# A two-layer backbone on one core: centred values, guards in place of four waits for transfers, and other prices for transfers in the kernel's planner

## The chip, the cores and the metric

The kernel runs on one core of a Trainium2 chip. A core has TensorE (PE in the profile; its weight loads are the row PEld), VectorE (DVE), ScalarE (ACT), GpSimd (POOL) and SyncE (SP), each with a queue of its own that is worked off in order, and 16 DMA engines. DMAs of this kernel are issued by SP and POOL. The metric is device time in microseconds (us), the median of several runs.

## The reference

The model has two layers over 512 tokens (x) and a context of 256 tokens, of width 1024. Layer 0 is an RWKV-7 mixer with a scan forwards and backwards over 32 heads of 64, layer 1 a Hyena mixer with long convolutions. What matters here, cut down:

```python
def adaln(cond, w, b):
    return jnp.split(jax.nn.silu(cond) @ w + b, 3, axis=-1)

def rwkv7_scan(...):            # per head, S is 64 x 64
    s = s * w_t + (s @ a_t) b_t + v_t k_t ;  y_t = s @ r_t

def rwkv7_readout(y, bonus, gate, p, dtype):
    mean = jnp.mean(y, axis=-1, keepdims=True)
    var = jnp.mean(jnp.square(y - mean), axis=-1, keepdims=True)
    yn = merge_heads((y - mean) * lax.rsqrt(var + RWKV_GN_EPS))
    yn = yn * p['ln_w'] + p['ln_b']
    return ((yn + merge_heads(bonus)) * jax.nn.silu(gate)).astype(dtype)

def hyena_filters(length, p):   # three sine layers of width 64, then f_w4 and a window
    hdn = sin(...) ; filt = hdn @ p['f_w4'] ; return filt * window
```

The output y of the scan is linear in the values v, along the 64 channels over which the readout takes its mean: the mean of y is what the same scan would give for the mean of v.

## The kernel before, in words

The order of the instructions is worked out while the kernel is built. Generators (each a piece of the work: a product, a readout, a chain) sit in lanes; `run` (L255) asks each live generator for its next instruction, and emits the one that a model of the chip (class Model, L72) lets start first. A lane's `bias` is added to that time, so that a negative one brings its work forward. `Model.note` (L142) keeps a clock for each engine and one clock `mem` for all transfers: a transfer of `size` elements takes size / 62e3 us on it and lands 0.6 us later. The chip does not know these clocks: each engine runs its instructions in the order of emission, and waits where one is not ready. A generator that yields nothing waits in the plan without an instruction being emitted.

The stages in the profile: up to 240 us the norm, adaln's first parts and the products for the values; from 240 to 740 us the products for keys, r and gates, decays, the key side and a part of the triangular inverses; then the scan, and beside it the readouts and the output product; from 1606 us the last readouts, the filters of layer 1 and the residual; then layer 1.

- `adaln` (L478) computes silu(c) times the weights, in blocks of columns. In the lane `mods1` it takes 128 columns at a time, in two loads of four row blocks each into one buffer `aw`: load, four matmuls into a PSUM bank of kind `ad`, load, four more, one more with the bias, a copy, and a second use of the bank. From the scan on, kind `ad` is the same single bank as kind `pm` (L1283), which the merges, the readouts and filter_base use as well. The bank is held from the first matmul to the copy, across the second load.
- `inverse` (L1229) loads blocks of the triangular systems by six transposing DMAs (lt<-ld, pieces of 32 elements) and works on them on DVE.
- `merge` (L1325) puts the inverses of one pair of heads together; the chain of a round (two pairs) needs its two merges.
- `chain` (L1483) is the scan: 8 rounds of 12 steps, each four groups of small matmuls with copies between them. `fetch` and `prep` (L1372, L1410) bring its operands (ar, bk) and, for the first group of a pair, transpose the values by matmuls with `ident` (L1425).
- `gemms` with `g_out` (L943) makes the gates; each product is emptied by the lane `evac` (L881). From the scan on one PSUM bank serves them.
- `readout` (L1568) takes y of one pair: product with `mean64` for the mean, subtraction, square, product with `mean64` for the variance, Ln, Exp, multiplications, then the bonus and the gate. `operand` and `out_part` make the output product of it.
- `filter_base` (L580) computes the three sine layers during the scan and stores them to DRAM (`hkd`). After the scan `filter_loads` (L560) loads f_w4 and the windows, `filter_parts` (L612) loads hkd twice into one tile, rounds it (ACT), takes the remainder (DVE) and multiplies, and `filter_transforms` makes the filter's transform.

Of the kernel before, what the change touches and what calls it, by code (L numbers as in the profile page):

```python
# [17 lines left out]
P = 128  # L18
# [20 lines left out]
for _n, _w in [("sel", 2), ("one32", 32), ("ones", 128), ("selg", 128), ("ident", 128), ("mean64", 128), ("ones64", 128), ("mask", 256),  # L39
               ("scanm", 12 * 65)]:  # L40
    CST[_n] = (_o, _w)
    _o += _w
# [29 lines left out]
class Model:  # L72
# [41 lines left out]

    def free(self, eng, ap, write):
# [26 lines left out]
    def note(self, op):  # L142
# [3 lines left out]
        if fn == "dma_start":  # L146
# [6 lines left out]
            self.mem = max(self.mem, go + 0.9) + size / 62e3  # L153
            end, e = self.mem + 0.6, "D"
# [85 lines left out]
def net_kernel(ctx: ExitStack, tc: tile.TileContext, I, out, dbg=None):  # L240
# [188 lines left out]
    ident, ones, mean64, ones64 = K("ident"), K("ones"), K("mean64"), K("ones64")  # L429
# [47 lines left out]

    def adaln(lps, ap, width, nk, bufs, row, aw=None):  # L478

        todo = [(l, part, cb, k) for l, part in lps for cb in range(D // width) for k in range(0, KT, nk)]  # L480
        w = []

        def load(l, part, cb, k):
            t = aw(len(w)) if aw else tl(ap, "aw", [P, nk, width], bufs)
            w.append(t)
            src = I["ada_w"][l, k * P:(k + nk) * P, part * D + width * cb:part * D + width * (cb + 1)]
# [3 lines left out]
        for n, (l, part, cb, k0) in enumerate(todo):  # L490
# [4 lines left out]
            if n + bufs - 1 < len(todo):  # L495
                yield load(*todo[n + bufs - 1])
            if k0 == 0:
                b, t = yield from get("ad")
                b = b[:, 0:width]
            for k in range(k0, k0 + nk):  # L500
# [44 lines left out]
    hkd = tl(dr, "hkd", [64, TX])  # L545
# [14 lines left out]
    def filter_loads():  # L560

        w4 = I["l1_f_w4"].rearrange("k (b c) -> k b c", b=2)
        for i, cb in funits:
# [8 lines left out]
            floads.append((wf, wft, win))  # L572
# [7 lines left out]
    def filter_base():  # L580
# [27 lines left out]
        yield dma(out=hkd, in_=hd)  # L608
# [3 lines left out]
    def filter_parts():  # L612
# [3 lines left out]
        hk, hd = filter_tile("hk", [P, TX], dt=F32R), filter_tile("hd", [P, TX], tag="ev")  # L616
        for hf in range(2):
            yield dma(out=hd[64 * hf:64 * hf + 64], in_=hkd)
        yield S.activation(out=hk, in_=hd, func=AF.Copy)
        yield V.tensor_tensor(out=hk[64:128], in0=hd[64:128], in1=fr(hk[64:128]), op=SUB)  # L620
        for n, (i, cb) in enumerate(funits):
            while len(floads) <= n:
                yield
            wf, wft, win = floads[n]
# [785 lines left out]
    def prep(p, g):  # L1410
# [6 lines left out]
        if g == 0:  # L1417
            vw, VT, vtok = vals[p]
            for c0 in range(0, NC, 8):
                n = min(8, NC - c0)  # L1420
                b, t = yield from get("pb")
                for i in range(n):
                    for h in range(2):
                        yield T.matmul(b[HR[1 - h], i * C:(i + 1) * C], lhsT=vw[:, (c0 + i) * C:(c0 + i + 1) * C], rhs=ident[:, HR[h]], start=True, stop=True)
# [143 lines left out]
    def readout(p, yb):  # L1568
# [10 lines left out]
        b, t = yield from get("pm")  # L1579
        yield T.matmul(b, lhsT=mean64, rhs=y, start=True, stop=True)  # L1580
        yield V.tensor_tensor(out=y, in0=y, in1=b, op=SUB)
        t[0] = True
# [502 lines left out]
```

## Time and profile before

| what | us |
|---|---|
| median of 3 runs | 2297.0 (2293.72 to 2299.8) |
| the profiled execution | 2309.6 |
| its span | 2307.7 |
| PE busy | 2032.2 (88%) |
| DVE busy | 1650.6 (72%) |
| ACT busy | 1058.7 (46%) |
| mean granted clock of PE | 0.941 of full speed |

The profile shows one execution. The span is the time from its first to its last instruction. A busy time is the time in which an engine executes; what an engine waited for is inferred from its semaphores. An fp32 matmul of 128 columns by 512 appears as two records. A wait for a transfer (DMA) is named by the tile that is loaded and the tensor that it comes from, as aw<-ada_w. PE and its weight loads are listed apart, and a stall often shows in both.

### The profile page before, as it was taken

Reading aid. Unit: us, or ns where it says so; the run is one execution under the profiler, and the core shown is the slowest. Engines: PE = TensorE matmul, PEld = TensorE weight load, DVE = VectorE, ACT = ScalarE, POOL = GpSimd, SP = SyncE. Lnnn points to the kernel's source line nnn. Section 1 sums busy time; section 2 is a strip of 40 time slices with the busy share of each in tenths; the row PEclk is TensorE's granted clock in tenths of the full one; section 3 lists DMA queues with packets and bytes.
Section 4 is the critical chain, followed back from the end, with each engine's and each line's share of the span. In section 5 each row is a group of like instructions: output and inputs, shape, how many; then the busy total and the mean of one; then the engine's idle time right before and its main releaser. Section 6 shows DMA issues by size and latency. Waiting matters only on the chain.

```text
span 2307.7 us, 53374 instructions
## 1 busy us (share of the span) xinstructions
PE 2032.2 (88%) x21710; PEld 1606.1 (70%) x21710; DVE 1650.6 (72%) x2646; ACT 1058.7 (46%) x1881; POOL 375.8 (16%) x583
## 2 busy tenths in 40 slices
PE   6699899999877688788988988888779999999997
PEld 2488777777655466666777767776457788878786
DVE  1956379989789678856676766776677676758676
ACT  2534578879663233334444443533563333333333
POOL 0400100000000432323334242211232000000000
PEclk8699999999989897989999999999889999999999
DMA  7145757795777975668655556453575323233232
GB/s 244 43 174 187 235 177 244 249 261 182 227 218 267 181 201 131 151 159 174 147 151 145 139 147 154 133 149 92 181 214 178 131 70 110 78 96 96 85 123 76
DMA packets 317564, 369.26 MB, mean 160 GB/s; under 512 B 132387, under 2 KB 203630, under 8 KB 317320
## 3 DMA queue, kind: packets, MB, share of 16 engines
q1 hardware_dynamic: 303832, 330.34, 49.6%
q0 software_dynamic: 13488, 35.52, 5.3%
q8 instruction: 171, 2.80, 0.5%
q14 instruction: 73, 0.60, 0.1%
HBM read 262.79 MB, written 102.17 MB: 158 GB/s over the span
## 4 chain that ended last, share of the span: by engine, by line
PE 52%; DVE 19%; DMA 12%; issue 5%; ACT 3%; SPq 2%; POOL 1%; DVEq 0%; ACTq 0%; POOLq 0%
PE ps L58 52%; SPq L58 2%; DVE wlo L58 2%; DVE bk L58 2%; DVE ar L58 2%; DMA aw<-ada_w 2%; DMA ar<-zd 2%; DMA wraw<-wg 2%; DVE ltm L58 1%; DVE ta L58 1%; DVE sv L58 1%; DVE lt L58 1%; DMA ar<-ard 1%; DVE cvv L58 1%; DMA tt<-td 1%
## 5 line engine op out<-in xcount | busy, mean ns | idle before, releaser
L58 PE MATMUL ps<-m,whi 128*128 128x512 f32 (+1 forms) x1536 | 423.3, 377 | 35.1 <-DVE ro L58 11.2
L58 ACT ACTIVATE whi<-wraw 128x512 fp32r<-128x512 f32 x320 | 200.8, 628 | 388.6 <-PE ps L58 274.8
L58 DVE TENSOR_TENSOR wlo<-wraw,whi 128x512 fp32r<-128x512 f32 x320 | 225.8, 707 | 200.8 <-ACT whi L58 198.6
L58 PEld LDWEIGHTS ps<-m,whi 128*128 128x128 f32 x1536 | 264.7, 197 | 92.1 <-ACT m L58 13.5
L58 PE MATMUL ps<-m,wlo 128*128 128x512 f32 (+1 forms) x768 | 247.7, 373 | 4.9 <-DVE wlo L58 4.8
L58 PE MATMUL ps<-ar,bk 128*64 128x64 f32 (+2 forms) x4096 | 220.2, 243 | 31.6 <-DVE ar L58 11.9
L58 PEld LDWEIGHTS ps<-ar,bk 128*64 128x64 f32 (+1 forms) x4096 | 186.7, 141 | 54.4 <-issue 22.0
L58 PE MATMUL ps<-h1h,whi 128*128 128x512 f32 x512 | 201.4, 393 | 2.6 <-ACT whi L58 1.9
L58 PE MATMUL ps<-h1l,whi 128*128 128x512 f32 x512 | 200.2, 391 | 0.7 <-DVE h1l L58 0.7
L58 PE MATMUL ps<-h1h,wlo 128*128 128x512 f32 x512 | 200.6, 392 | 0.0
L58 PEld LDWEIGHTS ps<-m,wlo 128*128 128x128 f32 x768 | 134.1, 197 | 31.5 <-DVE wlo L58 6.7
L58 DVE TENSOR_TENSOR ar<-ps,cst 64x512 f32<-64x512 f32 (+1 forms) x192 | 115.1, 600 | 28.3 <-PE ps L58 22.3
L58 POOL TENSOR_TENSOR sc<-sc,gam 128x256 f32<-128x256 f32 x80 | 55.5, 694 | 421.6 <-DVE sv L58 413.5
L58 PEld LDWEIGHTS ps<-h1h,whi 128*128 128x128 f32 x512 | 96.3, 188 | 22.5 <-ACT whi L58 2.3
L58 PEld LDWEIGHTS ps<-h1h,wlo 128*128 128x128 f32 x512 | 96.4, 188 | 20.3 <-DVE wlo L58 0.7
L58 PEld LDWEIGHTS ps<-h1l,whi 128*128 128x128 f32 x512 | 96.3, 188 | 20.3 <-DVE h1l L58 1.2
L58 PE MATMUL ps<-sv,bt 128*64 128x64 f32 x1408 | 90.7, 238 | 12.1 <-DVE sv L58 6.4
L58 ACT ACT_TABLE_LOAD x75 | 96.2, 1283 | 5.2 <-PE ps L58 3.1
L58 DVE TENSOR_TENSOR ltm<-lt 128x90 f32<-128x90 f32 (+14 forms) x120 | 81.1, 676 | 20.8 <-DMA lt<-ld 17.5
L58 PEld LDWEIGHTS ps<-sv,bt 128*64 128x64 f32 x1408 | 68.6, 143 | 38.6 <-ACT sv L58 14.1
L58 PE MATMUL ps<-xs,tt 128*64 128x64 f32 x1536 | 68.5, 233 | 28.6 <-DVE xs L58 26.7
L58 POOL DMA_DIRECT2D tt<-td x144 | 87.1, 609 | 9.9 <-DMA zd<-tt 4.9
(292 smaller groups left out, 4382.6 us busy)
## 6 DMA issues: line engine op xcount, KB each, us to landing
wraw<-wg SPq DMA_DIRECT2D x128, 256.0 KB
wraw<-w SPq DMA_DIRECT2D x128, 256.0 KB
aw<-ada_w SPq DMA_DIRECT2D x96, 256.0 KB
bkd<-bk SPq DMA_DIRECT2D x32, 768.0 KB
ard<-ar SPq DMA_DIRECT2D x32, 640.0 KB
ar<-ard SPq DMA_DIRECT2D x128, 128.0 KB
ar<-zd SPq DMA_DIRECT2D x128, 128.0 KB
wraw<-w_out SPq DMA_DIRECT2D x64, 256.0 KB
```

What stands on the lines that cost most here:

```text
L58: return getattr(self.eng.eng, self.fn)(*self.a, **self.k)
```

## The change

- The transposition of the values multiplies by `cent` = I - mean over each head's 64 channels, in place of I. Values and y are then centred; the readout's product for the mean and its subtraction are left out, and the variance's product takes `ones64` with a scale of 1/64 in the Ln.
- `adaln` remembers for each load the PE clock of the plan plus 8.0 us, and (but in its early use) yields nothing until that clock is reached: before it takes the bank, and before each group of matmuls.
- `filter_base` makes the rounded half and the remainder of the sine layers itself and stores both; `filter_parts` has one load, on POOL's queue, and neither ACT's nor DVE's instruction. Its first unit also yields nothing until 9.0 us of the plan's PE clock after the first weights' load.
- Transfers are priced by the length of their contiguous pieces (the shorter of the two sides): 27e3 elements per us up to 32 elements, 50e3 up to 64, 66e3 beyond, and each lands 1.2 us later.
- The lane `evac` has the bias -0.5 from the scan on.

```diff
@@ -36,7 +36,7 @@
 
 CST = {}
 _o = 0
-for _n, _w in [("sel", 2), ("one32", 32), ("ones", 128), ("selg", 128), ("ident", 128), ("mean64", 128), ("ones64", 128), ("mask", 256),
+for _n, _w in [("sel", 2), ("one32", 32), ("ones", 128), ("selg", 128), ("ident", 128), ("cent", 128), ("ones64", 128), ("mask", 256),
                ("scanm", 12 * 65)]:
     CST[_n] = (_o, _w)
     _o += _w
@@ -112,6 +112,16 @@
                 hi += s * (n - 1)
         return p0, p0 + pn, lo, hi
 
+    @staticmethod
+    def run(ap):
+
+        n = 1
+        for s, m in reversed(ap.ap if ap.space == DRAM else ap.ap[1:]):
+            if s != n and m > 1:
+                break
+            n *= m
+        return n
+
     def free(self, eng, ap, write):
         tr = self.tracks.get(self.key(ap))
         if not tr:
@@ -150,8 +160,9 @@
                 self.hw = max(self.hw, start) + 0.53
                 self.clock[e], go = start + 0.06, self.hw
             size = min(math.prod(outs[0].shape), math.prod(ins[0].shape)) if ins else 0
-            self.mem = max(self.mem, go + 0.9) + size / 62e3
-            end, e = self.mem + 0.6, "D"
+            run = min(self.run(v) for v in (*outs, *ins))
+            self.mem = max(self.mem, go + 0.9) + size / (27e3 if run <= 32 else 50e3 if run <= 64 else 66e3)
+            end, e = self.mem + 1.2, "D"
         else:
             end = self.clock[e] = start + self.price(e, op, outs[0], start)
             if outs[0].shape[0] < P:
@@ -426,7 +437,7 @@
         o, w = CST[name]
         return cst[:, o:o + w]
 
-    ident, ones, mean64, ones64 = K("ident"), K("ones"), K("mean64"), K("ones64")
+    ident, ones, cent, ones64 = K("ident"), K("ones"), K("cent"), K("ones64")
     mask = K("mask").rearrange("p (z a t) -> p z a t", z=2, a=2)
     par = tl(con, "par", [P, len(PAR), NP])
     do(dma(out=par, in_=I["par"]))
@@ -475,14 +486,17 @@
     do(V.tensor_scalar(out=cth, in0=cth, scalar1=0.5, scalar2=0.5, op0=MUL, op1=ADD))
     do(V.tensor_tensor(out=cpad[:, :, 0:2], in0=c2, in1=cth, op=MUL))
 
+    AWL = 8.0
+
     def adaln(lps, ap, width, nk, bufs, row, aw=None):
 
         todo = [(l, part, cb, k) for l, part in lps for cb in range(D // width) for k in range(0, KT, nk)]
-        w = []
+        w, at = [], []
 
         def load(l, part, cb, k):
             t = aw(len(w)) if aw else tl(ap, "aw", [P, nk, width], bufs)
             w.append(t)
+            at.append(model.clock["T"] + AWL)
             src = I["ada_w"][l, k * P:(k + nk) * P, part * D + width * cb:part * D + width * (cb + 1)]
             return dma(out=t, in_=src.rearrange("(k p) c -> p k c", p=P))
         for t in todo[:bufs - 1]:
@@ -494,9 +508,13 @@
                 yield dma(out=adab, in_=I["ada_b"][l:l + 1, part * D + width * cb:part * D + width * (cb + 1)])
             if n + bufs - 1 < len(todo):
                 yield load(*todo[n + bufs - 1])
+            while not aw and k0 == 0 and model.clock["T"] < at[n]:
+                yield
             if k0 == 0:
                 b, t = yield from get("ad")
                 b = b[:, 0:width]
+            while not aw and model.clock["T"] < at[n]:
+                yield
             for k in range(k0, k0 + nk):
                 yield T.matmul(b[32 * (k % 4):32 * (k % 4) + 32, :], lhsT=cpad[:, k, :], rhs=w[n][:, k - k0], start=k < 4, stop=k > 4)
             if k < KT - 1:
@@ -542,7 +560,7 @@
     td = [[tl(dr, f"td{z}_{b}", [2, UB, 32, 32]) for b in range(NB)] for z in range(2)]
 
 
-    hkd = tl(dr, "hkd", [64, TX])
+    hkd = tl(dr, "hkd", [P, TX])
     kfd = [tl(dr, f"kfd{b}", [P, 2, 4, 512]) for b in range(4)]
 
     def filter_tile(name, shape, bufs=1, dt=F32, tag=None):
@@ -569,7 +587,7 @@
             for hf in range(2):
                 yield FQ.dma_start(out=wf[64 * hf:64 * hf + 64], in_=w4[:, :, cs])
             win = []
-            floads.append((wf, wft, win))
+            floads.append((wf, wft, win, model.clock["T"] + 9.0))
             for a in range(4):
                 while winring.full():
                     yield
@@ -605,7 +623,11 @@
             yield V.scalar_tensor_tensor(out=hd, in0=nn, scalar=-6.28125, in1=hd, op0=MUL, op1=ADD)
             yield V.scalar_tensor_tensor(out=hd, in0=nn, scalar=-(2 * math.pi - 6.28125), in1=hd, op0=MUL, op1=ADD)
             yield S.activation(out=hd, in_=hd, func=AF.Sin)
-        yield dma(out=hkd, in_=hd)
+        hh = tl(rv, "hh", [64, TX], dt=F32R, tag="vx")
+        yield S.activation(out=hh, in_=hd, func=AF.Copy)
+        yield dma(out=hkd[0:64], in_=fr(hh))
+        yield V.tensor_tensor(out=hd, in0=hd, in1=fr(hh), op=SUB)
+        yield dma(out=hkd[64:128], in_=hd)
         toks[0][0] = toks[1][0] = True
         fbase.append(1)
 
@@ -613,15 +635,12 @@
 
         while not fbase:
             yield
-        hk, hd = filter_tile("hk", [P, TX], dt=F32R), filter_tile("hd", [P, TX], tag="ev")
-        for hf in range(2):
-            yield dma(out=hd[64 * hf:64 * hf + 64], in_=hkd)
-        yield S.activation(out=hk, in_=hd, func=AF.Copy)
-        yield V.tensor_tensor(out=hk[64:128], in0=hd[64:128], in1=fr(hk[64:128]), op=SUB)
+        hk = filter_tile("hk", [P, TX], dt=F32R)
+        yield G.dma_start(out=hk, in_=hkd.bitcast(F32R))
         for n, (i, cb) in enumerate(funits):
-            while len(floads) <= n:
+            while len(floads) <= n or (n == 0 and model.clock["T"] < floads[0][3]):
                 yield
-            wf, wft, win = floads[n]
+            wf, wft, win, _ = floads[n]
             sw = wf[:, 0, :]
             yield V.tensor_tensor(out=sw, in0=wf[:, 0, :], in1=wf[:, 1, :], op=SUB if i else ADD)
             swh, swl = filter_tile("swh", [P, 512], dt=F32R), filter_tile("swl", [P, 512], dt=F32R)
@@ -1415,13 +1434,14 @@
             yield
         AR, BK, ARB, BT, tok, btok = got_[p, g]
         if g == 0:
+
             vw, VT, vtok = vals[p]
             for c0 in range(0, NC, 8):
                 n = min(8, NC - c0)
                 b, t = yield from get("pb")
                 for i in range(n):
                     for h in range(2):
-                        yield T.matmul(b[HR[1 - h], i * C:(i + 1) * C], lhsT=vw[:, (c0 + i) * C:(c0 + i + 1) * C], rhs=ident[:, HR[h]], start=True, stop=True)
+                        yield T.matmul(b[HR[1 - h], i * C:(i + 1) * C], lhsT=vw[:, (c0 + i) * C:(c0 + i + 1) * C], rhs=cent[:, HR[h]], start=True, stop=True)
                 yield copy((V, S), VT[:, c0:c0 + n], b[:, 0:n * C].rearrange("p (c d) -> p c d", d=C))
                 t[0] = True
             vtok[0] = True
@@ -1576,15 +1596,11 @@
         yield dma(out=vx, in_=vd[p][:, SX])
         yield G.tensor_tensor(out=bo, in0=bo, in1=vx, op=MUL)
         y = yb[:, p % 2].rearrange("p c t -> p (c t)")
-        b, t = yield from get("pm")
-        yield T.matmul(b, lhsT=mean64, rhs=y, start=True, stop=True)
-        yield V.tensor_tensor(out=y, in0=y, in1=b, op=SUB)
-        t[0] = True
         s2 = tl(rv, "s2", [P, TX])
         yield S.activation(out=s2, in_=y, func=AF.Square)
         b, t = yield from get("pm")
-        yield T.matmul(b, lhsT=mean64, rhs=s2, start=True, stop=True)
-        yield S.activation(out=s2, in_=b, func=AF.Ln, bias=gneps)
+        yield T.matmul(b, lhsT=ones64, rhs=s2, start=True, stop=True)
+        yield S.activation(out=s2, in_=b, func=AF.Ln, scale=1.0 / 64, bias=gneps)
         t[0] = True
         yield S.activation(out=s2, in_=s2, func=AF.Exp, scale=-0.5)
         yield V.tensor_tensor(out=y, in0=y, in1=s2, op=MUL)
@@ -1680,6 +1696,7 @@
     G2BIAS = 0
     EPW = 0
     glane.bias = G2BIAS
+    evac.bias = -0.5
     pick["eps"] = EPW
     run([Lane([(passed, bring.out[:], rings["pb"].toks[2])]), Lane([(zeros,)]), *scans, *ends], lambda: over(glane, evac))
     gpc.close()
@@ -1995,7 +2012,7 @@
     put("ident", np.eye(P))
     put("ones", 1.0)
     same = (i[:, None] // 64 == i[None, :] // 64)
-    put("mean64", same / 64.0)
+    put("cent", np.eye(P) - same / 64.0)
     put("ones64", same)
     s, t = i[:, None] % 64, np.arange(64)[None, :]
     put("mask", np.concatenate([s < t, s <= t, s > t, s >= t], 1))
```

## Rows read from the trace of the kernel before

**Rows 1.** The page: the span, and busy time and share of each engine.

```profile
span 2307.7 us, 53374 instructions
...
PE 2032.2 (88%) x21710; PEld 1606.1 (70%) x21710; DVE 1650.6 (72%) x2646; ACT 1058.7 (46%) x1881; POOL 375.8 (16%) x583
```

**Rows 2.** Busy time by stage: stretch, length, engines (instructions), PE clock, DMA share, GB/s.

```profile
240.00:740.00 500.00, 449.81 (x3554) 343.80 (x3552) 425.54 (x568) 358.88 (x612) 15.78 (x51) 0.95 0.73 230
...
740.00:852.00 112.00, 83.67 (x941) 64.17 (x943) 78.41 (x125) 33.66 (x57) 46.24 (x60) 0.87 0.82 196
...
852.00:1606.00 754.00, 657.29 (x13318) 527.98 (x13315) 537.53 (x1016) 309.40 (x624) 227.84 (x381) 0.95 0.59 143
...
1606.00:1720.00 114.00, 75.65 (x296) 52.96 (x290) 76.21 (x114) 58.74 (x98) 32.66 (x28) 0.82 0.65 196
...
1850.00:2308.00 458.00, 439.65 (x2123) 366.53 (x2121) 314.79 (x517) 151.85 (x257) 5.39 (x4) 0.99 0.29 92
```

**Rows 3.** Waits of PE, whole run: total us, times, longest us.

```profile
PE ps L58 <- DMA aw<-ada_w: 31.3, 13, 12.8
```

**Rows 4.** Waits of PE for transfers from 240 to 740 us.

```profile
PE ps L58 <- DMA aw<-ada_w: 9.1, 7, 3.8
```

**Rows 5.** Waits of PE, then of DVE, from 740 to 852 us.

```profile
PE ps L58 <- DMA aw<-ada_w: 12.8, 1, 12.8
...
PE ps L58 <- DVE ro L58: 11.2, 4, 5.5
...
DVE ltm L58 <- DMA lt<-ld: 14.8, 1, 14.8
```

**Rows 6.** Waits of PE for transfers from 852 to 1606 us.

```profile
PE ps L58 <- DMA aw<-ada_w: 9.4, 5, 3.9
...
PE ps L58 <- DMA ar<-zd: 7.8, 8, 1.5
...
PE ps L58 <- DMA ar<-ard: 4.5, 3, 1.8
...
PE ps L58 <- DMA bk<-bkd: 3.5, 1, 3.5
```

**Rows 7.** Timeline after the scan: start, us, engine, instruction [idle before, releaser].

```profile
1609.85 1.11 SPq L58 DMA_DIRECT2D hd<-hkd  x2
...
1619.60 0.63 ACT L58 ACTIVATE hk<-hd 128x512 fp32r<-128x512 f32 x1 [14.54 <-DMA hd<-hkd]
...
1622.98 1.22 PE L58 MATMUL ps<-s,cst 128*128 128x512 f32 x1 [14.16 <-ACT s L58]
```

**Rows 8.** DMA issues: queue, count, KB each, median us to landing.

```profile
tfl<-fcl POOLq DMA_DIRECT2D x1, 512.0 KB, 8.8
```

**Rows 9.** Groups of instructions by shape: count, busy us, mean ns, idle before.

```profile
L58 PE MATMUL ps<-yb,cst 128*128 128x512 f32 x32 | 17.9, 642 | 2.0 <-ACT tt L58 1.8 <-DVE npo L58 0.2
...
L58 DVE TENSOR_TENSOR yb<-yb,ps 128x512 f32<-128x512 f32 x16 | 10.9, 680 | 0.6 <-PE ps L58 0.4
```

**Rows 10.** Timeline of the last readout.

```profile
1634.53 1.84 PE L58 MATMUL ps<-yb,cst 128*128 128x512 f32 x2
...
1638.36 0.63 ACT L58 ACTIVATE s<-yb 128x512 f32<-128x512 f32 x1 [1.95 <-DVE yb L58]
```

**Rows 11.** Timeline of SP's queue at the change of stage.

```profile
750.96 9.61 SPq L58 DMA_DIRECT2D lt<-ld  x6
...
762.81 0.39 SPq L58 DMA_DIRECT2D aw<-ada_w  x1
```

**Rows 12.** Timeline before the first step of the chain.

```profile
806.68 0.43 PE L58 MATMUL ps<-aw,cpad 128*32 128x128 f32 x8
...
823.75 0.15 DVE L58 SCALAR_TENSOR_TENSOR sc<-ps,npre 128x2 f32<-128x2 f32 x1
...
837.91 1.19 PE L58 MATMUL ps<-t,l 32*32 32x32 f32 x96
...
852.38 0.34 PE L58 MATMUL ps<-xs,tt 128*64 128x64 f32 x4
```

## The prediction

> **What bounds the kernel now.** I read the page first, then the busy times by stage, then the waits of TensorE (PE) stage by stage, then the timelines of the two places where PE stands longest. The page says that PE is busy for 88% of the span and VectorE (DVE) for 72% [rows 1]: no engine is full, so the stage decides. The table by stage [rows 2] shows four regimes. From 240 to 740 us (keys and decays) PE is busy for 449.8 of 500 us and DVE for 425.5: two engines share the bound, and a stall of one can hide behind the other. From 740 to 852 us (change to the scan) PE is busy for 83.7 of 112 us and its granted clock is 0.87. From 852 to 1606 us (the scan's chain, 96 steps) PE is busy for 657.3 of 754 us: 96.7 us of gaps, in a stage in which each step waits for the one before it. From 1606 to 1720 us (last readouts, filters, residual) PE is busy for 75.7 of 114 us, at a granted clock of 0.82. From 1850 us on PE is busy for 439.7 of 458 us at 0.99; the change leaves no operation out there, and I count nothing for it.
>
> Since every engine takes its instructions in the planner's order, an instruction that the planner believes ready and that is not stops all that is queued behind it. The waits for adaln's weight tile are of that kind: PE stands 31.3 us in 13 waits [rows 3].
>
> **The change part by part.** The sum is made in the profiled execution, 2309.6 us with what lies around its span of 2307.7 us [rows 1]; the median of the runs shown is 2297.0, so 12.6 us are taken off at the end.
>
> *Guards in adaln.* No instruction is added; the planner only withholds the matmuls until its PE clock is 8 us past the load's issue, so other PE work is put ahead. Of the 31.3 us, 9.1 lie between 240 and 740 us [rows 4], 12.8 in one wait between 740 and 852 us [rows 5], 9.4 in the scan [rows 6]. In the first stage DVE is 85% busy [rows 2], so a PE that runs earlier often finds DVE late next: I take 4 us (0 to 9.1). In the scan the chain's own small matmuls sit behind the stalled one, and little covers it: I take 7 (0 to 9.4). The 12.8 us wait is partly SP's doing: SP issues lt<-ld for 9.61 us from 750.96, and the load of aw goes out only at 762.81 [rows 11]. The planner counts its 8 us from where it thinks the load was issued, so the guard can miss some of it.
>
> *Prices.* Transfers in pieces of at most 32 elements go from 62 to 27 thousand elements per us, of at most 64 to 50, longer ones to 66, and each lands 0.6 us later. The six lt<-ld loads (65,536 elements each) were priced at 6 x 1.06 = 6.3 us and are now 6 x 2.43 = 14.6; on the chip DVE stood 14.8 us for them [rows 5]. So the planner will put other work ahead of that inverse. In the scan PE stands 7.8 + 4.5 + 3.5 = 15.8 us for ar and bk [rows 6]; those of ar are long pieces, whose price moves by 0.6 us only. I take 5 of the 15.8. A new order can also lose; no row prices that, and I bound it at 10 us in the scan, about a tenth of its 96.7 us of gaps.
>
> *evac.bias = -0.5 from the scan's start.* The evacuation of a gate tile is picked sooner on ScalarE (ACT) and DVE. PE stood 11.2 us in four waits for DVE's ro [rows 5], since one PSUM bank serves these products. With the 12.8 us this makes 24.0 us between 740 and 852 us. But this stage ends at the chain's first step, and what sets that is not PE: the second merge needs the one PSUM bank of kind pm, which adaln held from 806.68 to 823.75 us; the merge's first matmul came at 837.91, the chain's at 852.38 [rows 12]. I take 6 us, from 24.0 down to a loss of 17.1, one more such hold (806.68 to 823.75) ahead of the merge.
>
> *Centred values.* The values' transposing matmuls take another constant of the same shape: no cost. Each of 16 readouts loses one fp32 product (two records in the trace) and one DVE subtraction: 17.9/16 = 1.12 us of PE and 10.9/16 = 0.68 us of DVE [rows 9]. ACT's Ln takes a scale in place of the scaled constant: nothing. 14 readouts lie in the scan: 15.7 us of PE, off the chain itself but between its steps on the same queue. With PE 87% busy there I take half, 8 us (0 to 15.7). In the last readout they lie on the path: from the product at 1634.53 to the square at 1638.36 are 3.8 us [rows 10]; I take 3.
>
> *The filter's basis.* After the scan ACT waits 14.54 us for hd<-hkd, which SP issues behind the filter's own loads, and the readout's square stands behind it in ACT's queue: PE's next matmul comes after 14.16 us of nothing [rows 7]. Now the split is made long before, in filter_base (one ACT copy and one DVE subtraction of half a tile, at most 0.63 + 0.68 us by like rows [rows 7, 9], taken as nothing, in the chain's gaps; 1.3 if not), two stores go out where one did, and one load on POOL's queue brings hk. ACT and DVE no longer wait for it; PE does, and behind that the filter. A load that POOL issued there landed in 8.8 us [rows 8], so hk is there at about 1606 + 1 + 9 = 1616 us in place of 1619.60 + 0.63 = 1620.2: the filter gains 4 us, the readouts up to 14.2. The readouts lead to the output product and the residual, the filter has work to spare: nearer the 14.2, I take 10 (4 to 14.2). The guard on the first filter weights (9 us) ends at about the same time as the load and costs nothing more.
>
> A page speaks against part of this. The Trainium skill, "DMA: Bandwidth & Descriptors", section "Issuing engines are not separate DMA queues", says that transfers issued by SP, ACT or POOL run on the same 16 DMA engines and interleave. By that rule hk, with the filter's other loads in flight, would land no sooner than hd did; no row of before has this load on POOL. The sum would lose most of the 10 us (third rival).
>
> **The sum.** 4 (240 to 740) + 6 (740 to 852) + 7 + 5 + 8 = 20 (scan) + 10 + 3 = 13 (after it) = 43 us. 2309.6 - 43 = 2266.6, less 12.6: **2254 us**. All bounds at their best: 9.1 + 24.0 + 40.9 + 18.0 = 92 us, 2205; all at their worst: 0 - 17.1 - 10 + 4 - 1.3 = a loss of 24, 2321.
>
> **The rivals.**
> First, *other waits take over*: PE's stalls were cover for DVE, which is then late itself. For it: DVE is busy for 425.5 of 500 us and 78.4 of 112 us [rows 2]. Against it: the 14 us after the scan are idle on every engine. Gain 2 + 0 + 10 + 10 = 22 us: 2275.
> Second, *the prices do more*: most transfer waits of the scan go (9.4 + 15.8 us) with all of the readout's share (15.7), and the change of stage gives 12: 4 + 12 + 36 + 13 = 65 us, 2232.
> Third, *hk lands as late as hd did* and the filter binds after the scan: 1 + 3 = 4 us in place of 13, 34 in all: 2263.
> Fourth, *nothing much*: two stages give a little, a later start of the chain takes it back: 2297.
> Fifth, on the other side, *adaln keeps the bank*. A guarded second half holds pm for at least 8 us after its load is issued. The hold in the trace is 17.1 us [rows 12]; filter_base, the first two merges and the readouts want the same bank. If more holds fall ahead of the second merge, the chain starts later by 17.1 us each. The other gains are 4 + 20 + 13 = 37 us: from three holds on (51 us) it is slower. Four: 68 - 37 = 31 us lost, 2328; three: 2311. I price it at 2315. For it: two loads lie in each hold. Against it: this hold already had a load in it, and planned holds grow by a few us only.
>
> **How the numbers follow.** Forecast 2254 (2240 to 2268): 0.45. First rival 0.22, second 0.12, third 0.08, fourth 0.05, fifth 0.08. Runs of this kernel differ by about 0.3%, 7 us. Faster by more than that: 0.45 + 0.22 + 0.12 + 0.08 = 0.87; within: 0.05; slower: 0.08. The range takes in the first three rivals and stops below the fourth: 2224 to 2294.
>
> **What would show it.** PE's waits for aw after 240 us under 10 us; no wait of ACT for hd<-hkd and less than 9 us of PE idle after the scan; 32 records fewer of ps<-yb,cst; the chain's first step by 848 us and its 96 steps in under 740 us; ps<-m matmuls no longer waiting for ro. The prediction is wrong if the chain starts after 870 us, if adaln ends so late that the residual waits for it, or if the gaps of PE in the scan stay near 97 us.

## The result and the profile after

The changed kernel takes 2330.8 us (median; 2324.9 to 2335.0) where the kernel before takes 2298.4 beside it: 1.0122 times as long, 95% interval 1.0099 to 1.0145. It is slower, and the forecast of 2254 us and the range of 2224 to 2294 both miss. The profiled execution has a span of 2331.8 us, 24.1 more than before [rows 1]; the medians differ by 32.4 us, since the profiled execution of before, 2309.6 us, lies 11.2 above its median.

The page of the kernel after: the span, and busy time and share of each engine.

```profile
span 2331.8 us, 53247 instructions
...
PE 2028.5 (87%) x21678; PEld 1610.2 (69%) x21678; DVE 1650.6 (71%) x2633; ACT 1067.9 (46%) x1908; POOL 356.7 (15%) x555
```

PE has 32 records fewer than before and is busy 3.7 us less, so its idle time grew by 27.8 us. But the 32 records took 17.9 us [rows 9]: the records that stay took 14.2 us longer, at a mean granted clock of 0.934 in place of 0.941. The run a65 below makes the same 21,678 records in another order:

```profile
PE 2016.7 (88%) x21678; PEld 1602.1 (70%) x21678; DVE 1646.3 (72%) x2626; ACT 1070.0 (47%) x1906; POOL 367.6 (16%) x564
```

So a part of after's loss is PE busy for longer with the same work; the rest is waiting. How much of that part belongs to the order is open: f_cent and f_both below, of nearly one order, are busy for 2026.4 and 2017.5 us.

The stages of the kernel after, cut at the same events as in [rows 2] (columns as there).

```profile
240.00:750.00 510.00, 445.88 (x3503) 344.28 (x3502) 428.14 (x563) 357.15 (x613) 16.66 (x49) 0.94 0.70 220
750.00:868.00 118.00, 92.20 (x1017) 70.21 (x1015) 86.52 (x142) 38.24 (x64) 42.37 (x56) 0.87 0.86 209
868.00:1641.00 773.00, 653.81 (x13232) 526.90 (x13232) 520.07 (x990) 314.44 (x644) 215.95 (x361) 0.92 0.56 140
1641.00:1755.00 114.00, 76.54 (x313) 54.97 (x312) 82.13 (x116) 60.36 (x99) 31.06 (x28) 0.82 0.67 199
```

The chain's first and last step stand in one row of the view of the tile xs, of before and of after (durations in ns, least, median and most, then the first and the last start).

```profile
L58 PE MATMUL ps<-xs,tt x1536: 219/222/368, 852.4 to 1604.4; 128*64 128x64 f32 x192
```
```profile
L58 PE MATMUL ps<-xs,tt x1536: 216/222/370, 867.6 to 1639.8; 128*64 128x64 f32 x192
```

The chain starts 15.2 us later and its 96 steps take 772.2 us instead of 752.0, 20.2 more. From its last step to the end of the span are 692.0 us instead of 703.3, 11.3 less. 15.2 + 20.2 - 11.3 = 24.1. These are single executions; how far one row can move by itself is shown below.

**The waits that were to go have gone.** All waits for adaln's weight tile in the kernel after, whole run:

```profile
PEld ps L58 <- DMA aw<-ada_w: 7.8, 13, 1.0
```

The row is of weight loads; PE's matmuls have no such wait left. The longest is 1.0 us, where one of before was 12.8 [rows 3]. In the scan PE waits 2.7 + 2.3 = 5.0 us for ar and no longer for bk (before 15.8 [rows 6]). But other waits of PE have grown. From 852 to 1605 us of before, then from 868 to 1640 us of after (us, times, longest):

```profile
PE ps L58 <- DVE sv L58: 9.3, 20, 1.0
...
PE ps L58 <- DVE arb L58: 6.7, 5, 3.0
...
PE ps L58 <- DVE x L58: 2.4, 5, 0.9
```
```profile
PE ps L58 <- DVE sv L58: 23.7, 33, 3.6
...
PE ps L58 <- DVE arb L58: 9.7, 8, 2.9
PE ps L58 <- DVE x L58: 8.1, 16, 1.2
...
PE ps L58 <- DMA ar<-ard: 2.7, 3, 1.1
PE ps L58 <- DMA ar<-zd: 2.3, 2, 1.5
```

For sv, arb and x PE waits 41.5 us where it waited 18.4. The gaps of PE between the first and the last step grow from 96.7 [rows 2] to 119.2 us. No operation that makes sv, arb or x is changed; what is different about them is the order that the planner gives, and the engine that it picks for some copies.

**A stall in the keys.** The timeline of the kernel after: SP issues the six lt<-ld over 23.88 us, and behind them in its queue stand the wraw<-wg for which ACT then waits.

```profile
645.28 23.88 SPq L58 DMA_DIRECT2D lt<-ld  x6
669.26 2.21 SPq L58 DMA_DIRECT2D wraw<-wg  x2
...
673.94 0.63 ACT L58 ACTIVATE whi<-wraw 128x512 fp32r<-128x512 f32 x1 [14.05 <-DMA wraw<-wg]
...
673.56 0.25 DVE L58 TENSOR_TENSOR ltm<-lt 128x90 f32<-128x90 f32 x1 [11.62 <-DMA lt<-ld]
```

The same place of before, 12.61 us for the same six:

```profile
629.36 12.61 SPq L58 DMA_DIRECT2D lt<-ld  x6
642.07 2.22 SPq L58 DMA_DIRECT2D wraw<-wg  x2
```

PE's waits from 600 to 700 us of after show what that cost; before has neither row there. The second comes later, at 697.84 us: DVE, working off the inverse that started late, reaches wlo only then.

```profile
PE ps L58 <- ACT whi L58: 12.3, 1, 12.3
PE ps L58 <- DVE wlo L58: 11.6, 1, 11.6
```

**After the scan** the stall of 14.16 us [rows 7] has another cause and nearly the same length. The kernel after, timeline:

```profile
1642.15 0.60 POOL L58 DMA_DIRECT2D hk<-hkd  x1 [9.90 <-DVE yb L58]
...
1646.73 0.50 SPq L58 DMA_DIRECT2D sg<-gd  x1
...
1655.44 0.69 DVE L58 SCALAR_TENSOR_TENSOR bo<-bo,sg 128x512 f32<-128x512 f32 x1 [5.17 <-DMA sg<-gd]
1656.17 0.63 ACT L58 ACTIVATE uh<-bo 128x512 fp32r<-128x512 f32 x1 [6.70 <-DVE bo L58]
1656.70 0.61 ACT L58 ACTIVATE s<-yb 128x512 f32<-128x512 f32 x1
1657.37 2.08 PE L58 MATMUL ps<-s,cst 128*128 128x512 f32 x2 [13.22 <-ACT s L58]
```

ACT no longer waits for hd, but the planner put the next readout's square (s<-yb) behind uh<-bo, which needs the gate tile sg; SP issued sg behind the filter's loads at 1646.73, and DVE could use it 8.7 us later. The stall also stands at another place: it is the second of the two readouts after the scan that waits, and its square starts 16.9 us after the chain's last step (1656.70 for 1639.8), where that of before came 34.0 us after it (1638.36 [rows 10] for 1604.4). So the stage is shorter although the stall is as long.

### The profile page after: what moved, and what is told of

It is laid out like the page before. It is cut to its first block, busy times and chain, and to the rows that moved or that the text cites. A ratio compares the mean times of both kernels' runs of the same rounds, so it can differ in the third digit from the quotient of the medians.

```text
span 2331.8 us, 53247 instructions
## 1 busy us (share of the span) xinstructions
PE 2028.5 (87%) x21678; PEld 1610.2 (69%) x21678; DVE 1650.6 (71%) x2633; ACT 1067.9 (46%) x1908; POOL 356.7 (15%) x555
## 5 line engine op out<-in xcount | busy, mean ns | idle before, releaser
L58 PE MATMUL ps<-ar,bk 128*64 128x64 f32 (+2 forms) x4096 | 218.6, 244 | 29.2 <-DVE ar L58 17.9
L58 PEld LDWEIGHTS ps<-h1h,wlo 128*128 128x128 f32 x512 | 96.1, 188 | 20.2 <-DVE wlo L58 0.8
L58 PE MATMUL ps<-sv,ar 128*64 128x64 f32 x1536 | 83.2, 240 | 13.2 <-DVE sv L58 10.3
```

The lines of the kernel that those rows point to most:

```text
L58: return getattr(self.eng.eng, self.fn)(*self.a, **self.k)
```

## The experiments

Each run is set beside runs of the kernel before on the same chip; the ratio is to these, so it is not the quotient of two rows of the table. The chain's start, its length and the time from its last step to the end of the span come from the profiled execution, by the row of xs,tt shown above. Three things are to be kept in mind when they are read.

A profiled execution can lie 14 us off the median (f_cent 2308.2 for 2294.0). And the start moves by itself: in f_cent and f_both every engine has before's instructions in before's order until the scan is under way (the first difference in any queue lies at 878 us), and yet their chains start 1.2 and 9.7 us earlier. A difference of under some 10 us in that column says nothing. The rows of f_cent, then of f_both:

```profile
L58 PE MATMUL ps<-xs,tt x1536: 218/222/370, 851.2 to 1605.7; 128*64 128x64 f32 x192
```
```profile
L58 PE MATMUL ps<-xs,tt x1536: 219/222/370, 842.7 to 1587.5; 128*64 128x64 f32 x192
```

Last, start and steps trade with each other: what a plan leaves undone before the first step, it does between the steps.

| run | what it is | us | ratio to before | chain starts | 96 steps | last step to end |
|---|---|---|---|---|---|---|
| before | | 2298.4 | 1 | 852.4 | 752.0 | 703.3 |
| after | all five edits | 2330.8 | 1.0122 (1.0099-1.0145) | 867.6 | 772.2 | 692.0 |
| a65 | after, long pieces at 65 | 2297.5 | 0.9980 (0.9965-0.9995) | 859.4 | 743.8 | 691.9 |
| a67 | after, long pieces at 67 | 2296.4 | 0.9981 (0.9963-0.9999) | 850.4 | 751.7 | 691.3 |
| n61 | before, 61 for 62 | 2345.2 | 1.0215 (1.0182-1.0248) | 881.1 | 762.1 | 702.3 |
| n63 | before, 63 for 62 | 2333.7 | 1.0162 (1.0135-1.0188) | 861.3 | 770.5 | 699.2 |
| n64 | before, 64 for 62 | 2321.3 | 1.0089 (1.0061-1.0118) | 847.5 | 769.7 | 703.4 |
| prices | price list alone | 2321.8 | 1.0074 (1.0052-1.0096) | 836.6 | 780.2 | 699.4 |
| p65 | same, 65 for 66 | 2324.5 | 1.0111 (1.0080-1.0142) | 867.3 | 763.2 | 700.0 |
| p67 | same, 67 for 66 | 2336.1 | 1.0161 (1.0136-1.0186) | 860.1 | 763.7 | 705.2 |
| no_prices | all but the price list | 2308.1 | 1.0026 (1.0005-1.0046) | 849.4 | 750.9 | 702.7 |
| np61 | same, 61 for 62 | 2315.6 | 1.0068 (1.0048-1.0089) | 860.3 | 762.8 | 692.2 |
| np63 | same, 63 for 62 | 2303.1 | 1.0023 (1.0010-1.0036) | 847.7 | 757.8 | 693.7 |
| cent_hk | centred values, filter's basis | 2298.8 | 0.9972 (0.9950-0.9994) | 847.9 | 766.7 | 685.1 |
| ch61 | same, 61 for 62 | 2356.2 | 1.0240 (1.0209-1.0271) | 887.9 | 774.6 | 694.0 |
| ch63 | same, 63 for 62 | 2319.2 | 1.0074 (1.0044-1.0103) | 865.7 | 765.1 | 693.1 |
| guards | adaln's guards alone | 2329.4 | 1.0103 (1.0058-1.0147) | 822.9 | 806.0 | 703.6 |
| f_cent | centred values, order frozen | 2294.0 | 0.9991 (0.9962-1.0019) | 851.2 | 754.5 | 700.6 |
| f_both | and the filter's basis, order frozen | 2285.8 | 0.9945 (0.9929-0.9961) | 842.7 | 744.8 | 693.8 |
| f_aw | before without waits for aw, order frozen | 2294.0 | 0.9954 (0.9930-0.9978) | 841.6 | 745.9 | 704.1 |

No run has the bias alone. The first question was which of the five edits loses the time. Theory 1 was the price list, theory 2 the guards in adaln (the fifth rival), theory 3 that any new order of the planner moves the time.

**Edits alone and left out.** prices and guards are before with that edit and nothing else, cent_hk is before with two edits, no_prices is after with this line back:

```diff
-            self.mem = max(self.mem, go + 0.9) + size / (27e3 if run <= 32 else 50e3 if run <= 64 else 66e3)
-            end, e = self.mem + 1.2, "D"
+            self.mem = max(self.mem, go + 0.9) + size / 62e3
+            end, e = self.mem + 0.6, "D"
```

> The kernel before with the new prices of transfers alone (rates by piece length and a landing of 1.2 us). Theory 1, the price list: it makes the planner hold back what hangs on tt, l and lt for longer than the chip needs; the chain starts at 860 us or later (before 852.4) and its 96 steps take 765 us or more (before 752.0); without the gains of the other parts the time is 2325 to 2350 us. Theory 2, adaln's guards hold the bank: the prices alone give 2285 to 2300. Theory 3, any new order moves the time by up to 0.7% either way: 2282 to 2315.

> The kernel after with the old prices (62 thousand elements per us, landing 0.6 us); guards, centred values, the filter's basis and the bias stay. Theory 1, the price list: the loss goes and the gains stay: the chain starts by 860 us, its steps take under 755 us, 2260 to 2280 us. Theory 2, the guards: still 2310 to 2330. Theory 3, order: 2280 to 2315.

> The kernel before with adaln's two guards of 8 us alone. Theory 1, the price list: the guards are harmless, PE's waits for aw after 240 us fall from 31.3 to under 10 us, 2280 to 2297 us. Theory 2, the guards hold the pm bank: merges and the chain come later, adaln's last matmul at 1300 us or later (before 1177.4), 2310 to 2330. Theory 3, order: 2282 to 2315.

> The kernel before with the centred values and the filter's basis (split early, one load on POOL's queue) alone. By the prediction's terms 8 us in the scan, 3 in the last readout and 10 after the scan: 2272 to 2280 us, whatever theory holds for the rest. Theory 3, order: 2275 to 2310, and the time from the chain's last step to the end is 10 us shorter than the 703 us of before in any case.

None of the theories that blame one edit holds as stated. The price list alone loses 0.74%, less than theory 1 wanted, and leaving it out brings after to 1.0026, not under 0.99. The guards alone lose 1.03%, and 2329.4 us is inside theory 2's range; adaln's last matmul comes at 1419.7 us, as it said. But the runs no_prices, a65 and a67 have the guards too, end adaln at 1350 to 1387 us, and take within 0.3% of before's time: the guards do not cost 1% in every order. cent_hk gains 18.2 us after the last step (685.1 for 703.3) and loses 14.7 in the chain, which the two edits only relieve.

Theory 2 also wanted a later chain, and the row says 822.9 us, 29.5 earlier than before. That start is half a step. PE in guards, between 820 and 861 us:

```profile
822.56 0.43 PE L58 MATMUL ps<-aw,cpad 128*32 128x128 f32 x8
822.91 0.45 PE L58 MATMUL ps<-xs,tt 128*64 128x64 f32 x8
...
850.09 1.06 PE L58 MATMUL ps<-t,l 32*32 32x32 f32 x96
...
859.66 0.48 PE L58 MATMUL ps<-xs,tt 128*64 128x64 f32 x4 [3.81 <-ACT tt L58]
```

Eight of the sixteen records of the first step run early; the others wait for tt, which the second merge (ps<-t,l) fills, and that starts 12.2 us later than in before (837.91 [rows 12]); the round's second merge is needed for the second half of a step only. The second step starts at 871.2 us, in before at 866.5. So a merge was late here. In before one hold of the bank by adaln lies between the first two merges, 17.1 us [rows 12]; in guards also one, from 822.56 to the copy of sh at 843.21, 20.7 us; in after one of 16.1 us (826.71 to 842.79). prices has the same half step: 8 records from 836.6, the others from 859.9. And 13,689 records of PE lie between the first and the last step of guards where before has 13,302: a part of its 806.0 us is work that before did earlier.

Theory 3 is right in its sign only. Its ranges were too narrow: prices, guards, n61, n63 and ch61 below lie above them, a65 and a67 under them.

**The order alone.** n61, n63 and n64 are the kernel before with one number changed. The work is the same (21,710 PE records in each); the order differs, and with it which engine some copies go to, since the planner picks that too.

```diff
-            self.mem = max(self.mem, go + 0.9) + size / 62e3
+            self.mem = max(self.mem, go + 0.9) + size / 61e3
```

> The kernel before with one number changed: the planner prices a transfer at 61 thousand elements per us in place of 62. Same instructions, only their order can differ; nothing of the change is in it. Theory 3 (any new order moves the time, and before stands on a good one): slower than before by 0.4 to 1.2%, 2308 to 2330 us, with 765 us or more for the chain's 96 steps (before 752.0). Theories 1 and 2 (a part of the change is what costs): within 0.3% of before.

> The same with 63 thousand elements per us. Theory 3: it differs from before by 0.3% or more, more likely slower (2305 to 2325 us). Theories 1 and 2: within 0.3%.

> The kernel before with 64 thousand elements per us in place of 62, nothing else. Third draw of an order beside before's (61 gave 2345.2, 63 gave 2333.7 us). If before's order is a lucky one among many (theory 3): again slower by over 0.5%, 2310 to 2350. If the two were accidents and the price itself matters little: 2293 to 2306.

The three lose 2.15, 1.62 and 0.89% (46, 34 and 19 us by the medians) for a price that moved by 1.6 to 3.2%. n61 loses 28.7 us before the chain's first step and 10.1 in it, n64 starts 4.9 earlier and loses 17.7 in it. There is no one place, even with 10 us allowed for the start. The rows of xs,tt of n61 and of n64:

```profile
L58 PE MATMUL ps<-xs,tt x1536: 219/222/371, 881.1 to 1643.2; 128*64 128x64 f32 x192
```
```profile
L58 PE MATMUL ps<-xs,tt x1536: 219/222/369, 847.5 to 1617.2; 128*64 128x64 f32 x192
```

**The edits in a frozen order.** For f_cent and f_both the planner goes on counting the operations that fall away, and they are only not issued; what is new is issued with an operation that it already counts.

```diff
+def ghost(op, emit=lambda: None):
+    op.emit = emit
+    return op
...
-        yield T.matmul(b, lhsT=mean64, rhs=y, start=True, stop=True)
-        yield V.tensor_tensor(out=y, in0=y, in1=b, op=SUB)
+        yield ghost(T.matmul(b, lhsT=ones64, rhs=y, start=True, stop=True))
+        yield ghost(V.tensor_tensor(out=y, in0=y, in1=b, op=SUB))
...
-            yield dma(out=hd[64 * hf:64 * hf + 64], in_=hkd)
+            yield ghost(dma(out=hd[64 * hf:64 * hf + 64], in_=hkd[0:64]), [G.dma_start(out=hk, in_=hkd.bitcast(F32R)).emit, lambda: None][hf])
```

> The kernel before with centred values, the order frozen: the planner still counts the readout's mean product and subtraction, and they are only not issued. So this is before's order less 64 instructions, 32 PE records and 16 DVE. The prediction's term: 8 us of the scan and 3 of the last readout, 11 us: 2286 to 2292 us beside before's 2300. If the planner's reordering is what ate the gains (theory 3), the chain's 96 steps take 740 to 748 us here. If the readout's work lies in gaps anyway, 2296 to 2300.

> The same with the filter's basis too, its order frozen as well: the split and its two stores go out where the one store did, and one load on POOL's queue takes the place of the two loads of SP and the copy and subtraction behind them. The prediction's term: 10 us more than the run with centred values alone, all after the chain's last step: 2274 to 2284 us, 685 to 692 us from the last step to the end (before 703.3). If the load lands as late as before, or the next load (sg<-gd) binds: 2286 to 2292.

f_cent cannot be told from before. f_both is 0.55% faster (0.39 to 0.71), 12.6 us, and has the shortest time of the study. It leaves out one thing of the filter's basis: the guard of 9.0 us on its first unit. Its timeline after the scan:

```profile
1592.28 1.12 PE L58 MATMUL ps<-s,cst 128*128 128x512 f32 x2 [1.24 <-ACT s L58]
...
1597.29 0.80 PE L58 MATMUL ps<-swh,hk 128*128 128x512 f32 x1 [3.88 <-ACT swh L58]
...
1600.00 0.38 SPq L58 DMA_DIRECT2D sg<-gd  x1
```

Here the square does not stand behind sg. PE waits 1.24 us for it and 3.88 for the filter's weights, 5.1 in place of 14.16, as the prediction's step wanted. In after a new stall of 13.22 us stands there, and that is no accident of its order: all nine kernels with the filter's basis in their plan have it, from 11.49 us (cent_hk) to 13.91 (ch63), and in each the square stands behind uh<-bo, which needs sg. The row of cent_hk:

```profile
1630.67 2.07 PE L58 MATMUL ps<-s,cst 128*128 128x512 f32 x2 [11.49 <-ACT s L58]
```

Whether the guard on the first unit puts it there, or the plan without the two loads of hd, no run separates.

**What the guards could gain at most.** f_aw is before in its own order, with each late load of aw (all but the first of adaln's second part) sent to an unused place, while the matmuls read the first tile. The modulations that it computes are thus not the model's. The edit of the load:

```diff
-            return dma(out=t, in_=src.rearrange("(k p) c -> p k c", p=P))
+            return ghost(dma(out=t, in_=src), dma(out=dump, in_=src).emit) if late else dma(out=t, in_=src)
```

> The kernel before in its own order, with the waits for adaln's weight tile taken away: every load of aw but the first of the second part of adaln goes to an unused place in DRAM, and the matmuls read the first tile (the modulations are computed from wrong weights; the work and the issues of transfers are the same). This bounds what the guards could gain. The prediction's terms: 4 us in the keys, some of the 6 at the change to the scan, 7 in the scan: 2281 to 2290 beside 2299. If other waits take over: 2293 to 2300. More than that (under 2280): the waits held up more than PE.

0.46% (0.22 to 0.70), 10.6 us, for 31.3 us of waits [rows 3]: by the time, a third of them was on the path. PE has none of these waits left in f_aw; others are longer there, as ACT's longest wait for wraw<-wg, 16.4 us where it was 4.8.

**More orders of after.** One number of the price list:

```diff
-            self.mem = max(self.mem, go + 0.9) + size / (27e3 if run <= 32 else 50e3 if run <= 64 else 66e3)
+            self.mem = max(self.mem, go + 0.9) + size / (27e3 if run <= 32 else 50e3 if run <= 64 else 65e3)
```

> The kernel after with the price of long pieces at 65 thousand elements per us in place of 66, nothing else: another draw of its order. Theory 3: it scatters like before's neighbours, over 10 us or more, and as the two parts that hold in a frozen order are in it (13.6 us), around 2325: 2300 to 2345. Theory 1 (the price list itself makes every plan worse): the mean of the draws after stands above that of the draws before (2340).

> The same with 67 thousand elements per us: 2300 to 2345 under theory 3, mean of the draws over 2340 under theory 1.

Both are 1.4% faster than after and 0.2% faster than before. So after's loss is not a property of its edits, but of the order that one number of the price list gives them. Their chains start at 859.4 and 850.4 us and take 743.8 and 751.7 us.

**Does the price list, or do the guards, move the mean?** The same small steps of a price in kernels with other sets of edits:

> The kernel after with the old prices, at 61 thousand elements per us in place of 62: everything but the price list, another draw. If the price list harms every plan: 2285 to 2310. If only the draw counts, the mean of this cell stands between 2300 and 2330, and this run anywhere from 2290 to 2345.

> The same at 63. If the price list harms: 2285 to 2310. If it helps: over 2320, since the draws of after with it have a mean of 2308. If only the draw counts: 2290 to 2345.

> The kernel before with the price list alone, long pieces at 65 thousand elements per us: another draw of the run prices (2321.8). If the list helps by itself: under 2320, below before's own draws at 61, 63 and 64 (mean 2333). If it harms: over 2335. If only the draw counts: 2300 to 2345.

> The same at 67: under 2320 if the list helps, over 2335 if it harms, 2300 to 2345 if only the draw counts.

> Centred values and the filter's basis with the old price at 61 thousand elements per us: the run cent_hk with another draw of the order. If these two parts give 0.55% in every order, this run lies near n61 (1.0215) less 0.0055 or, if each edit draws anew, anywhere from 0.995 to 1.016. If the guards and the bias gain besides, the mean of this column (cent_hk 0.9972, this, ch63) stands above 1.0039, the mean with them; if not, at or below it.

> The same at 63 thousand elements per us: near n63 (1.0162) less 0.0055 if order and edit add up, anywhere from 0.995 to 1.016 if each edit draws anew; the column's mean as said for ch61.

ch61 is outside what was expected of it on either ground: 1.0240, over n61.

Means of three orders each, as change against before: no edit +1.55% (2.15, 1.62, 0.89); price list +1.15% (0.74, 1.11, 1.61); centred values and filter's basis +0.95% (-0.28, 2.40, 0.74); all but the price list +0.39% (0.26, 0.68, 0.23); all +0.28% (1.22, -0.20, -0.19). Within a set the runs scatter by 0.8% (root of the mean variance of the five), so a mean is known to about 0.5%. The price list moves its pairs by -0.40 and -0.11%: nothing that these runs can tell from zero. Centred values and basis stand 0.60% under no edit, near f_both (0.55%), guards and bias another 0.56% lower, near f_aw (0.46%), and all five edits 1.27% under no edit, some 29 us. Each of these differences is known to about 0.65% only, so the 0.60 and the 0.56 could be zero. And the set without an edit leaves out before's own order, while the other sets keep their first price: with it in, no edit stands at 1.17%, centred values and basis 0.21% under it, all five edits 0.89%. So a gain of the five edits in the mean of the orders is not shown; what is shown is f_both.

## Why the prediction was wrong, point by point

**The step that failed** is the one on the new order: "A new order can also lose; no row prices that, and I bound it at 10 us in the scan". Set against f_both, which has two of after's edits in before's order, after is 1.0122/0.9945 = 1.018 times as long: the order, with what guards, prices and bias do through it, costs some 41 us, four times the bound, and perhaps not only in the scan: in the profiles after loses 20.2 us in the chain and 15.2 before it, 9.8 of these before the first memset of xs (769.7 for 759.9 us), where the keys end; of the 15.2 some 10 could be the execution. The runs price the term that no row of before could: before's order has the best time of 17. Each of the 16 others, with 0.55% added back where it holds centred values and basis, is slower than before's, by 0.27 to 2.95%, 1.2% (27 us) in the mean; the nearest, cent_hk with 0.27%, is within what the intervals leave open. That after stood on a poor order among its neighbours is bad luck: with a price of 65 or 67 in place of 66 the same edits are 0.2% faster than before. The forecast took waits out of that order as if it stayed; three of the five edits work only by changing it, and the two others change it too.

**The gains that were costed**, each by its own run:
- *Centred values*: taken as 8 + 3 = 11 us; f_cent shows 2 (a loss of 4 to a gain of 9): the share of one half was too much. Why is not shown. The work may have lain in gaps of PE; in the profiled execution PE is busy only 5.8 us less (2026.4 for 2032.2) where the removed records took 17.9, so the others took longer. The loss of 32 records was right, and the Ln with its scale takes what it took, 688 ns.
- *The filter's basis*: taken as 10 us; f_both against f_cent shows 0.9945/0.9991, 10.6. It holds in other orders too: from the last step to the end are 693.0 us in the mean of the ten kernels of the table that have it (and centred values), 702.1 in the ten that have not, 9.1 of the 13 us forecast for this stage; no_prices is the only one of the first ten above 700. Two things inside it were wrong. The load: hk landed 5.0 us after its issue in after and 4.6 in f_both, not in 9; the row it was priced by is of a load of 512 KB [rows 8], and hk has 256. It was not late, so the third rival is out. And the next wait was not looked for: with hd gone the readout's square waits for sg, 13.22 us in after, a term that the sum does not have. The guard on the first unit, counted as costing nothing, may have a share in it.
- *Guards*: 4 + 7 us and a part of 6; about 10.6 (5 to 16) is what f_aw leaves them to gain. f_aw takes the waits away in before's order; the guards put other work in their place, so this is a bound by likeness.
- *Prices*: 5 us; ar and bk lost 10.8 us of waits, and no time that can be shown came of it.
- *Change of stage*: 6 us gained were forecast; 5.4 are lost in after's profile, less than one execution can move the start. The aw wait of 12.8 went, but PE waited 11.6 for ro as before [rows 5], 5.1 for wraw<-wg, and DVE 11.5 for lt<-ld. The bias did not free ps<-m from ro.

Together the frozen orders show 12.6 + 10.6 = 23 us where 43 were forecast, if the two add up. That is near the first rival's 22, other waits taking over, though not by its terms. So without the order too the sum was about twice what the runs show, apart from the 5 us of the prices and the bias, which no frozen run has.

The issue-to-landing rows (KB, median us) of hk in after and in f_both:

```profile
hk<-hkd POOLq DMA_DIRECT2D x1, 256.0 KB, 5.0
```
```profile
hk<-hkd POOLq DMA_DIRECT2D x1, 256.0 KB, 4.6
```

In both, SP issued the filter's own loads at the same moment. The Trainium skill, "DMA: Bandwidth & Descriptors", section "Issuing engines are not separate DMA queues", says that transfers of all issuers interleave on the same engines. These rows do not show hk held up, as the prediction drew from it. They do not speak against the rule either: hk goes out 0.5 us after the first of the filter's loads (SP's wf at 1641.67), where hd went out 3.5 us after it, behind six loads (1609.85 for 1606.32). Whether the place or the queue made the difference, no run separates.

**The fifth rival** was on the right side with a mechanism that the runs do not bear out. Its price of 2315 is nearer than the forecast. It wanted three or four more holds of the bank ahead of the second merge; after has one between the first two merges, of 16.1 us, where before has one of 17.1, and after's first merge, ahead of it, is already 19.4 us later (808.32 for 788.91). In guards alone the merge does come 12.2 us later, behind one hold of 20.7, but a65 and a67 have the guards and take less time than before. Its chance of 0.08 stood for one mechanism; the order as a whole was the rival to price, and n61 to n64 would have given it most of the chance.

**The tests named**: waits for aw under 10 us, right; 32 records fewer, right; no wait of ACT for hd, right, but 13.22 us of PE idle after the scan where under 9 were said; the first step by 848 us and steps under 740 us, wrong (867.6 and 772.2), the first step short of the 870 that was to refute; ps<-m free of ro, wrong; and the gaps of PE in the scan, named as what would make it wrong, went up.

**What stays open** is why before's order is better than its neighbours. They lose at different places, so no single wait explains them, and the runs only count them. Open is also how much of each loss is PE's records taking longer. Whether the guards and the bias gain their half per cent, and the price list anything, would take more orders of each.

## What to carry to other kernels

Where a list scheduler orders the instructions by prices, every edit that touches a price, a due time or the length of an operation draws a new order, and that draw can outweigh the edit: here it is worth 0.3 to 3% against 0.5% of direct gain. Cost the draw as a term of its own, wider than any single wait, and look for it with a step of 1 to 2% in a number that means nothing. Do not read a stage from its first instruction alone: half a step that runs early makes it look early. Judge an edit by freezing the order (count what is not issued) or by the mean of several orders, and ship the edit in the best order found: here centred values and the filter's basis in before's order, 0.55% faster.

## What the runs showed of the hardware

SP's time to issue one transfer of the same form varies widely. The view of the tile lt, on SP from 450 to 860 us, before and after (ns, least, median and most):

```profile
L58 SPq DMA_DIRECT2D lt<-ld x22: 585/1685/4632, 485.4 to 859.0; - x22
```
```profile
L58 SPq DMA_DIRECT2D lt<-ld x20: 597/1678/8817, 488.2 to 857.6; - x20
```

One issue takes 0.6 to 8.8 us, and what stands behind it in SP's queue waits as long. What decides between the two was not tried. Order and chance of the execution are not told apart for the 8.8 us; in the frozen orders the six issues that take 12.61 us in before take 12.69 (f_cent) and 11.89 (f_both), so the 23.88 us of after is more than these executions scatter.

PE's busy time is not fixed by its work. The same 21,710 matmul records in f_aw, then in guards:

```profile
PE 2021.8 (88%) x21710; PEld 1600.6 (70%) x21710; DVE 1651.1 (72%) x2646; ACT 1058.1 (46%) x1881; POOL 374.2 (16%) x583
```
```profile
PE 2047.5 (88%) x21710; PEld 1626.3 (70%) x21710; DVE 1650.8 (71%) x2637; ACT 1071.5 (46%) x1899; POOL 372.7 (16%) x575
```

The mean granted clocks of these executions are 0.947 and 0.931. Whether the clock alone makes the 25.7 us, no run separates.
